# Which queue stores go out of: ScalarE's finished tiles on ScalarE's own DMA queue, in a hybrid attention and mLSTM encoder layer

## The chip, the cores and the metric

The kernel runs on one core of one Trainium2 chip. The metric is the device time of one execution in microseconds (us). The engines have these names in the profile: PE is TensorE (matmuls; PEld is its weight loads), DVE is VectorE, ACT is ScalarE, POOL is GpSimd, and SP is SyncE, which does no arithmetic here and only issues DMA transfers. "SPq" and "ACTq" are the sequencers of an engine: they wait, branch and issue transfers while the engine itself computes nothing.

## The reference

One encoder layer over two sequences, of 1024 and of 2048 tokens, each with the same 16 meta tokens ahead, at a model width of 1024:

```python
xn = _rmsnorm(h, g_pre)
proj = xn @ w_in + b_in.astype(xn.dtype)
na_q, na_k, na_v, na_z, ml_qk, ml_v, ml_z, ml_o, ml_g, mg = jnp.split(proj, SPLIT_IDX, axis=-1)
ya = _neighbourhood_attention(na_q.reshape(hd), na_k.reshape(hd), na_v.reshape(hd), na_rpb)
ya = (ya.reshape(B, L, NA_WIDTH) * jax.nn.silu(na_z)) @ w_a
yb = (_mlstm_branch(ml_qk, ml_v, ml_g, ml_o, ml_conv_w, ml_head_g) * jax.nn.silu(ml_z)) @ w_b
ga, gb = jnp.split(jax.nn.sigmoid(mg), 2, axis=-1)
y = (ga * ya + gb * yb) @ w_out
return h + _rmsnorm(y, g_post)
```

The projection is 1024 by 6672. The first branch is attention over a window of 8 by 16 grid positions, 8 heads of 64; the second a bidirectional mLSTM in chunks, 4 heads of 128. All is in float32.

## The kernel before

**Tiling.** A float32 product is made of three matmuls on a high and a low part of each operand (`mm3`, lines 144 to 146; written out by hand at lines 412 to 414 and 1304 to 1306). ACT makes the high part by a rounding copy, VectorE the low part as the difference. Tokens run in halves of 512. A projection column block is either feature-major (`fm_half` with `fm_evac`: 128 columns by 512 tokens) or token-major (`tm_unit` with `tm_store`: 128 tokens by 256 or 264 columns). Products gather in one of three `pj` banks of PSUM, are evicted to an SBUF tile (`st`, four buffers; `stT`, four buffers), and then stored to a scratch tensor in DRAM, from which a later stage loads them in its own layout.

**Two strands.** `dense` makes the projections and the final products in the order of `PLAN`; `sparse` makes the mLSTM and the attention of both sequences in the order of `STEPS`. `run` weaves them: each `yield` of the sparse strand has a price, and dense work of that price is put behind it. So TensorE's order is written out by hand, and between one step of the attention and the next stand dense matmuls that give ACT and VectorE time. In the profile the first mLSTM lies between about 300 and 780 us, the first attention from 780 to 1193, the second mLSTM from 1193 to 2015, the second attention from 2015 to about 2850; the final products (`final`) begin at about 1515 and end the span.

**Queues.** Only TensorE's order is fixed by hand. The instructions of the other engines are put in order by the framework's scheduler, and each engine takes its own in that order: an instruction that waits holds all behind it on its engine. The framework also sets all semaphore waits. Nearly every transfer, load or store, is issued by SP (2352 of them); POOL issues 14, for constants of the attention.

**The places of the change**, all of them stores of a tile whose last writer is ACT:

- `wpump`, line 240: a weight block is loaded once from the input, split by ACT (`hi`, line 233) and by VectorE or POOL (`lo`, line 236), used, and both parts are kept in DRAM for the next time that block is needed (loaded at line 231). 68 blocks.
- `fm_evac`, lines 348 and 350: mLSTM queries and keys (`MQ`, `MK`), written by line 343. The loads are at line 843. Where a half carries the meta tokens, these are stored for the other sequence too (line 350).
- `fm_evac`, line 356: attention queries (`NQ`, written by line 333), keys (`NK`, line 343), the attention's gate (`NZ`, which VectorE writes last, line 339) and the output gates (`GT`, line 341). They are loaded at lines 550, 633 and 1267.
- `tm_store`, line 452: the mLSTM's output gate `TO`, after ACT's tanh in place (line 451); loaded at line 1170.
- `ml_norm`, `turn`, line 1208: the mLSTM's normalised result `YB`, copied out of PSUM by ACT (line 1205); loaded at line 1245.

Other stores keep their queue: those of tiles that VectorE writes last (lines 241's low part, 439, 449, 456 to 468, 710, 918, 1111, 1377).

**The steps that the prediction speaks of.** The attention works on units of one head and 16 grid columns: scores (lines 664, 665), bias and row maximum (DVE, 668), exponential (ACT, 672), scaling (DVE, 681), transposes (PE, 689), split of the transposed weights (ACT 691, DVE 692), product with the values (PE, 701) and its eviction (ACT, 705). The loads of the next head (`na_prep`, lines 550 to 637, and the bias at line 606) are issued as a burst. The mLSTM's loads stand at lines 843, 889, 998 and 1005; its decay rows `um` (line 1005) are used by VectorE at line 1043; `ktl` (line 956) is the low part of its transposed keys. `mx` is the row maximum, `prb` the exponentials, `kd` the high part of the attention's keys.

Of the kernel before, what the change touches and what calls it, by code (L numbers as in the profile page):

```python
# [9 lines left out]
F32 = mybir.dt.float32  # L10
# [7 lines left out]
P = 128  # L18
# [3 lines left out]
NM = 16  # L22
# [7 lines left out]
C_NQ, C_NK, C_NV, C_NZ = 0, 512, 1024, 1536  # L30
C_MQ, C_MK, C_MV, C_MZ, C_MO, C_GA, C_GB = 2048, 2560, 3072, 3584, 4096, 4624, 5648
# [79 lines left out]
class K:  # L111
# [107 lines left out]
    def wpump(self):  # L219


        nc, wp = self.nc, self.wp
        self.wload()
        while self.wraw and self.wout < NBW:
            key, raw, nk, w = self.wraw.popleft()
            n = nk * w
            hi = wp.tile([P, 4 * WU], F32R, name="whi", bufs=NBW)
            lo = wp.tile([P, 4 * WU], F32R, name="wlo", bufs=NBW)
            if raw is None:
                for x, d in zip((hi, lo), self.wkept[key]):  # L230
                    nc.sync.dma_start(x[:, :n].bitcast(F32), d[:, :])
            else:
                nc.scalar.activation(hi[:, :n], raw[:, :n], AF.Copy)
                self.nu += 1
                eng = nc.vector if self.nu > 4 else nc.gpsimd
                eng.tensor_tensor(lo[:, :n], raw[:, :n], hi[:, :n].bitcast(F32), op=ALU.subtract)
                self.wkept[key] = []
                for x, part in ((hi, "h"), (lo, "l")):
                    d = self.dp.tile([P, n], F32, name=f"w{part}{len(self.wkept)}")
                    nc.sync.dma_start(d[:, :], x[:, :n].bitcast(F32))  # L240
                    self.wkept[key].append(d)
            self.wrdy.append([x[:, :n].rearrange("p (k c) -> p k c", k=nk) for x in (hi, lo)])
            self.wout += 1
            self.wload()
# [77 lines left out]
    def fm_evac(self, col, s, t0, meta, chunks, ps):  # L322

        nc, wp = self.nc, self.wp
        bi = (col // P) if col < 4608 else 36 + (col - 4624) // P
        bias = self.bfm[:, bi:bi + 1]
        st = wp.tile([P, HALF], F32, name="st", bufs=4)
        m = NM if meta else 0
        n = 512 + m
        for (c0, c1), p in zip(chunks, ps):  # L330
            o, q = st[:, c0:c1], p[:, :c1 - c0]
            if col < C_NK:
                nc.scalar.activation(o.rearrange("p (b r c) -> p r b c", r=8, b=4), q.rearrange("p (r b c) -> p r b c", r=8, b=4),
                                     AF.Identity, bias=self.bq8[:, bi:bi + 1], scale=0.125)
            elif C_NZ <= col < C_MQ:
                zb = wp.tile([P, HALF], F32, name="st", bufs=4)
                nc.scalar.activation(zb[:, c0:c1], q, AF.Identity, bias=bias)
                nc.scalar.activation(o, q, AF.Tanh, bias=self.bfh[:, bi:bi + 1], scale=0.5)
                nc.vector.scalar_tensor_tensor(o, o, 1.0, zb[:, c0:c1], op0=ALU.add, op1=ALU.mult)
            elif col >= C_GA:  # L340
                nc.scalar.activation(o, q, AF.Tanh, bias=self.bfh[:, bi:bi + 1], scale=0.5)
            else:
                nc.scalar.activation(o, q, AF.Identity, bias=bias)
        if C_MQ <= col < C_MV:
            dst = (self.MQ if col < C_MK else self.MK)
            h = (col % 512) // P
            lo = 0 if meta else NM + t0
            nc.sync.dma_start(dst[s][h][:, lo:lo + n], st[:, :n])
            if meta:
                nc.sync.dma_start(dst[1 - s][h][:, :NM], st[:, :NM])  # L350
            return
        if col >= C_GA:
            dst = self.GT[s][(col - C_GA) // P]
        else:
            dst = (self.NQ, self.NK, None, self.NZ)[col // 512][s][(col % 512) // P]
        nc.sync.dma_start(dst[:, t0:t0 + 512], st[:, m:n])
        if meta and C_NK <= col < C_NV:
            km = wp.tile([P, 64], F32, name="km", bufs=1)
            nc.gpsimd.memset(km, 0.0)
            nc.gpsimd.tensor_copy(km[:, 8:24], st[:, :NM])  # L360
            nc.gpsimd.tensor_copy(km[:, 32:48], st[:, :NM])
            nc.sync.dma_start(self.NKM[(col % 512) // P][:, :], km)
# [63 lines left out]
    def tm_store(self, col, wd, s, n, cnt, tok, st):  # L426
        nc, wp = self.nc, self.wp

        def rows(d, c0, c1, lo):
            return d[lo:lo + n * cnt, c0:c1].rearrange("(a p) c -> p a c", p=n)  # L430

        f = col % 512
        if C_MZ <= col < C_MO:
            th = wp.tile([P, 2, WU], F32, name="thT", bufs=1)
            nc.scalar.activation(th[:, :, :wd], st[:, :, :wd], AF.Tanh, scale=0.5)
            nc.vector.scalar_tensor_tensor(st[:, :, :wd], th[:, :, :wd], 1.0, st[:, :, :wd], op0=ALU.add, op1=ALU.mult)
            for a in range(2):
                nc.vector.tensor_tensor(st[:, a, :wd], st[:, a, :wd], self.hgt[:, 0, :], op=ALU.mult)
            nc.sync.dma_start(rows(self.SZ[s], f, f + wd, tok), st[:, :, :wd])
        elif col >= C_MO:  # L440
            c0 = col - C_MO
            no = min(wd, 512 - c0)
            if wd > no:
                g = wd - no
                if tok is None:
                    for q in range(2):
                        nc.sync.dma_start(self.GA[q][0:NM, :], st[:n, 0, no:wd])
                else:
                    nc.sync.dma_start(rows(self.GA[s], 0, g, NM + tok), st[:, :, no:wd])
            if tok is not None:  # L450
                nc.scalar.activation(st[:, :, :no], st[:, :, :no], AF.Tanh, scale=0.5)
                nc.sync.dma_start(rows(self.TO[s], c0, c0 + no, tok), st[:, :, :no])
        elif col >= C_MV:
            if tok is None:
                for q in range(2):
                    nc.sync.dma_start(self.MV[q][0:NM, f:f + wd], st[:n, 0, :wd])
            else:
                nc.sync.dma_start(rows(self.MV[s], f, f + wd, NM + tok), st[:, :, :wd])
        else:
            if tok is None:  # L460
                for lo in (8, 32):
                    nc.sync.dma_start(self.NVM[lo:lo + NM, f:f + wd], st[:n, 0, :wd])
            else:
                for a in range(cnt):
                    for r in range(2):
                        row = (tok + a * P) // 64 + r
                        dst = self.NV[s][:, row * 8:row * 8 + 8, f:f + wd]
                        nc.sync.dma_start(dst, st[r * 64:r * 64 + 64, a, :wd])
# [686 lines left out]
    def ml_norm(self, mp, s):  # L1155

        nc = self.nc
# [37 lines left out]
        def turn(i, e):  # L1195
            if i < 0:
                return
            hb = ld[i][e][0]
            if e == 0:
                rr[i] = mp.tile([P, 4, 2, P], F32, name="ybo", bufs=2)  # L1200
            yo = rr[i]
            pt = self.psum("tr", [P, 4, P])
            for h in range(4):
                nc.tensor.transpose(pt[:, h, :], hb[:, h], self.ident)
            nc.scalar.activation(yo[:, :, e, :], pt, AF.Copy)
            if e:
                for h in range(4):
                    nc.sync.dma_start(self.YB[s][h][:, 2 * P * i:2 * P * (i + 1)], yo[:, h].rearrange("p a b -> p (a b)"))
                ld.pop(i)
                rr.pop(i)  # L1210

# [2 lines left out]
        for i in range(N + 1):  # L1214
            if i < N:
                load(i + 1)
                yield from stats(i)
                yield A_N
            turn(i - 1, 0)
            if i < N:  # L1220
                norm(i, 0)
            yield A_N
            turn(i - 1, 1)
            if i < N:
                norm(i, 1)
            yield A_N
# [266 lines left out]
```

## Time and profile before

| | us |
|---|---|
| Median of three runs | 2937.11 (2936.93 to 2938.26) |
| The profiled execution's own time | 2935.2 |
| Its span, first to last instruction | 2933.4 |
| TensorE busy in the span | 2820.8 |
| ScalarE busy | 1288.7 |
| VectorE busy | 1747.6 |

A row of the list of groups or waits names an engine, a line, and a tile written and tiles read (`out<-in`, buffer numbers left out). A row of waits has in its end the total in us, how often, and the longest: `PE sm L701 <- DVE pts L692: 15.7, 12, 4.7` says that TensorE stood idle 12 times, 15.7 us in all, until line 692 had ended. `SPq L356 <- ACT st L341` is SP's sequencer, which could not issue line 356 before line 341 had ended. A row of a stage has its bounds and length, then busy us and instruction count of PE, PEld, DVE, ACT and POOL, then TensorE's granted clock, the busy share of the DMA engines and GB/s. A row for one line's issues has least, median and longest duration in ns, and first and last start. The chain in order of time has start, duration and what. A timeline row has start, duration, engine, line, operation, tiles and count, with the idle time before it and what ended that. The issue of a transfer is a row of SPq; its duration is that of issuing, not of the transfer, which goes on after it.

### The profile page before, as it was taken

Reading aid. Unit: us, or ns where it says so; the run is one execution under the profiler, and the core shown is the slowest. Engines: PE = TensorE matmul, PEld = TensorE weight load, DVE = VectorE, ACT = ScalarE, POOL = GpSimd, SP = SyncE. Lnnn points to the kernel's source line nnn. Section 1 sums busy time; section 2 is a strip of 40 time slices with the busy share of each in tenths; the row PEclk is TensorE's granted clock in tenths of the full one; section 3 lists DMA queues with packets and bytes.
Section 4 is the critical chain, followed back from the end, with each engine's and each line's share of the span. In section 5 each row is a group of like instructions: output and inputs, shape, how many; then the busy total and the mean of one; then the engine's idle time right before and its main releaser. Section 6 shows DMA issues by size and latency. Waiting matters only on the chain.

```text
span 2933.4 us, 49345 instructions
## 1 busy us (share of the span) xinstructions
PE 2820.8 (96%) x17488; PEld 2510.8 (86%) x17488; DVE 1747.6 (60%) x4722; ACT 1288.7 (44%) x3114; POOL 23.1 (1%) x107
## 2 busy tenths in 40 slices
PE   6999999999799999999999999989999999989998
PEld 6998898899689988888887998977888888879797
DVE  5233566556556665465568776565555557777843
ACT  4213546433344444456566554413444445435421
POOL 1000000000000000000000000000000000000000
PEclk9999999999899999999999999999999999999999
DMA  9655667656775654568679898488568658897875
GB/s 350 219 179 181 197 218 256 232 182 207 255 232 153 198 175 134 168 232 298 197 234 363 277 313 290 136 263 272 172 196 283 191 174 272 245 280 236 283 273 194
DMA packets 438760, 675.25 MB, mean 230 GB/s; under 512 B 52240, under 2 KB 253024, under 8 KB 438512
## 3 DMA queue, kind: packets, MB, share of 16 engines
q1 hardware_dynamic: 437392, 669.41, 70.1%
q0 software_dynamic: 1120, 2.69, 0.4%
q8 instruction: 137, 2.24, 0.3%
q14 instruction: 111, 0.91, 0.1%
HBM read 455.05 MB, written 216.90 MB: 229 GB/s over the span
## 4 chain that ended last, share of the span: by engine, by line
PE 83%; DMA 9%; DVE 5%; ACT 1%; issue 1%; SPq 1%; DVEq 0%; ACTq 0%
PE pj L144 15%; PE pj L145 15%; PE pj L146 15%; PE pj L412 6%; PE pj L413 6%; PE pj L414 6%; PE sm L701 3%; PE pj L1304 3%; PE pj L1306 3%; PE pj L1305 3%; PE tr L689 2%; DMA tg<-gt 2%; PE sc L665 1%; PE sc L664 1%; PE sm L146 1%; PE sm L145 1%
## 5 line engine op out<-in xcount | busy, mean ns | idle before, releaser
L144 PE MATMUL pj<-xh,whi 128*128 128x512 f32 (+1 forms) x1824 | 722.2, 396 | 2.4 <-DVE xl L310 2.2
L145 PE MATMUL pj<-xl,whi 128*128 128x512 f32 (+1 forms) x1824 | 701.3, 384 | 0.6 <-DVE xl L310 0.6
L146 PE MATMUL pj<-xh,wlo 128*128 128x512 f32 (+1 forms) x1824 | 699.8, 384 | 0.0
L412 PE MATMUL pj<-whi,xh 128*128 128x256 f32 (+3 forms) x1576 | 450.8, 286 | 0.0
L413 PE MATMUL pj<-wlo,xh 128*128 128x256 f32 (+3 forms) x1576 | 444.7, 282 | 0.0
L414 PE MATMUL pj<-whi,xl 128*128 128x256 f32 (+3 forms) x1576 | 444.2, 282 | 0.0
L146 PEld LDWEIGHTS pj<-xh,wlo 128*128 128x128 f32 x1824 | 344.6, 189 | 72.3
L144 PEld LDWEIGHTS pj<-xh,whi 128*128 128x128 f32 x1824 | 345.2, 189 | 57.3 <-DVE xl L310 2.6
L145 PEld LDWEIGHTS pj<-xl,whi 128*128 128x128 f32 x1824 | 345.9, 190 | 53.3 <-DVE xl L310 0.8
L412 PEld LDWEIGHTS pj<-whi,xh 128*128 128x128 f32 (+1 forms) x1576 | 294.3, 187 | 1.2
L413 PEld LDWEIGHTS pj<-wlo,xh 128*128 128x128 f32 (+1 forms) x1576 | 294.0, 187 | 1.1
L414 PEld LDWEIGHTS pj<-whi,xl 128*128 128x128 f32 (+1 forms) x1576 | 294.1, 187 | 0.9
L692 DVE TENSOR_TENSOR pts<-tr,pts 96x512 fp32r<-96x512 f32 (+2 forms) x192 | 132.2, 688 | 159.4 <-ACT pts L691 158.3
L672 ACT ACTIVATE prb<-sc,mx 128x384 f32<-128x384 f32 (+2 forms) x192 | 119.4, 622 | 238.2 <-DVE mx L668 234.1
L1304 PE MATMUL pj<-whi,mh 128*128 128x256 f32 x768 | 221.0, 288 | 0.4 <-DMA whi<-wh 0.4
L1306 PE MATMUL pj<-whi,mlo 128*128 128x256 f32 x768 | 217.6, 283 | 2.1 <-DVE mlo L1287 2.1
L1305 PE MATMUL pj<-wlo,mh 128*128 128x256 f32 x768 | 217.2, 283 | 0.0
L691 ACT ACTIVATE pts<-tr 96x512 fp32r<-96x512 f32 (+2 forms) x192 | 114.3, 595 | 170.0 <-PE tr L689 169.3
L421 DVE TENSOR_TENSOR stT<-pj,bb 128x256 f32<-128x256 f32 (+3 forms) x197 | 83.1, 422 | 145.3 <-PE pj L414 141.2
L144 PE MATMUL pj<-yh,whi 128*128 128x512 f32 x384 | 158.0, 412 | 11.0 <-DVE tg L1283 11.0
L668 DVE CUSTOM_DVE_ANT_1 sc<-sc,gt 128x384 f32<-128x384 f32 (+2 forms) x192 | 118.9, 619 | 73.2 <-PE sc L665 67.4
L146 PE MATMUL pj<-yh,wlo 128*128 128x512 f32 x384 | 153.4, 399 | 0.0
(234 smaller groups left out, 5067.5 us busy)
## 6 DMA issues: line engine op xcount, KB each, us to landing
whi<-wh SPq DMA_DIRECT2D x176, 512.0 KB
wlo<-wl SPq DMA_DIRECT2D x176, 512.0 KB
wh<-whi SPq DMA_DIRECT2D x64, 512.0 KB
wl<-wlo SPq DMA_DIRECT2D x64, 512.0 KB
wraw<-w_in SPq DMA_DIRECT2D x48, 512.0 KB
gt<-st SPq DMA_DIRECT2D x96, 256.0 KB
tg<-gt SPq DMA_DIRECT2D x96, 256.0 KB
xh<-xh SPq DMA_DIRECT2D x6, 2048.0 KB
```

The lines of the kernel that those rows point to most:

```text
L144: mm(out, ah, bh, start=start, stop=False)
L145: mm(out, ah, bl, start=False, stop=False)
L146: mm(out, al, bh, start=False, stop=stop)
L412: nc.tensor.matmul(o, xh, wh, start=k == 0, stop=False)
L413: nc.tensor.matmul(o, xh, wl, start=False, stop=False)
L414: nc.tensor.matmul(o, xl, wh, start=False, stop=k == KT - 1)
L668: nc.vector.tensor_tensor_reduce(out=so, in0=so, in1=gt[:, g0:g0 + ns, c0:c0 + 32], op0=ALU.add, op1=ALU.min, scale=-1.0, scalar=3.0e38, a ...
L672: nc.scalar.activation(pr_[:, :N].rearrange("p (b a c) -> p b a c", b=4, c=8), sc[:, :N].rearrange("p (a b c) -> p b a c", b=4, c=8), AF.E ...
L692: nc.vector.tensor_tensor(pts[:ks, :, 1, :], pt[:ks], pts[:ks, :, 0, :].bitcast(F32), op=ALU.subtract)
L1304: nc.tensor.matmul(o, mh[:, k, xs], wh, start=k == 0, stop=False)
L1305: nc.tensor.matmul(o, mh[:, k, xs], wl, start=False, stop=False)
L1306: nc.tensor.matmul(o, ml[:, k, xs], wh, start=False, stop=k == KT - 1)
```

## The change

Six stores call `nc.scalar.dma_start`, so that ACT's sequencer issues them into ACT's own queue, in the place of `nc.sync.dma_start`. In `wpump` only the high part moves. In `fm_evac` the attention's gate `NZ` (columns `C_NZ` to `C_MQ`) stays with SP, and so does the meta keys' tile `km`. The tiles, the transfers and all arithmetic stay.

```diff
-                    nc.sync.dma_start(d[:, :], x[:, :n].bitcast(F32))
+                    (nc.scalar if part == "h" else nc.sync).dma_start(d[:, :], x[:, :n].bitcast(F32))
...
+        q = nc.sync if C_NZ <= col < C_MQ else nc.scalar
         if C_MQ <= col < C_MV:
...
-            nc.sync.dma_start(dst[s][h][:, lo:lo + n], st[:, :n])
+            q.dma_start(dst[s][h][:, lo:lo + n], st[:, :n])
             if meta:
-                nc.sync.dma_start(dst[1 - s][h][:, :NM], st[:, :NM])
+                q.dma_start(dst[1 - s][h][:, :NM], st[:, :NM])
             return
...
-        nc.sync.dma_start(dst[:, t0:t0 + 512], st[:, m:n])
+        q.dma_start(dst[:, t0:t0 + 512], st[:, m:n])
...
                 nc.scalar.activation(st[:, :, :no], st[:, :, :no], AF.Tanh, scale=0.5)
-                nc.sync.dma_start(rows(self.TO[s], c0, c0 + no, tok), st[:, :, :no])
+                nc.scalar.dma_start(rows(self.TO[s], c0, c0 + no, tok), st[:, :, :no])
...
-                    nc.sync.dma_start(self.YB[s][h][:, 2 * P * i:2 * P * (i + 1)], yo[:, h].rearrange("p a b -> p (a b)"))
+                    nc.scalar.dma_start(self.YB[s][h][:, 2 * P * i:2 * P * (i + 1)], yo[:, h].rearrange("p a b -> p (a b)"))
```

By the counts of the profile of before these are 340 transfers: 68 at line 240, 48 at 348, 8 at 350, 144 at 356, 24 at 452 and 48 at 1208.

## The prediction

> **What bounds the kernel now.** I read the page's head and chain first, then the busy time by stage, then TensorE's own waits.
>
> ```profile
> span 2933.4 us, 49345 instructions
> PE 2820.8 (96%) x17488; PEld 2510.8 (86%) x17488; DVE 1747.6 (60%) x4722; ACT 1288.7 (44%) x3114; POOL 23.1 (1%) x107
> PE 83%; DMA 9%; DVE 5%; ACT 1%; issue 1%; SPq 1%; DVEq 0%; ACTq 0%
> ```
> ```profile
> 0.00:60.00 60.00, 36.72 (x272) 35.55 (x273) 35.11 (x70) 28.35 (x50) 8.56 (x22) 0.97 0.98 337
> 1340.00:1950.00 610.00, 591.22 (x3519) 521.45 (x3519) 409.80 (x1166) 320.13 (x880) 3.58 (x18) 0.99 0.78 260
> 2015.00:2456.00 441.00, 439.38 (x2197) 364.95 (x2197) 243.83 (x589) 210.27 (x443) 1.02 (x2) 1.00 0.68 210
> 2456.00:2933.00 477.00, 444.68 (x2853) 401.27 (x2852) 316.15 (x766) 178.38 (x452) 1.02 (x2) 0.97 0.80 256
> ```
>
> TensorE is busy for 96% of the span and carries 83% of the chain. Its idle time is 2933.4 - 2820.8 = 112.6 us: 23.3 in the first 60 us (almost all before the first real product), 32.3 after 2456, and about 57 between. The moved stores end at 2456 (the last output-gate store), so the last 32.3 us can change only through another order of the other engines' work. ACT, the fourth busy time of a stage row, is at most 320.13 / 610 = 52% busy in these rows: it has room, but it stands between TensorE's products and TensorE's next operands. A microsecond that TensorE loses is not won back, so what counts is which waits in front of it shrink or grow.
>
> ```profile
> PE pj L307 <- DVE xr L296: 22.5, 2, 18.2
> PE tr L1204 <- DVE hn L1193: 15.9, 2, 10.0
> PE sm L701 <- DVE pts L692: 15.7, 12, 4.7
> PE sc L664 <- ACT kd L644: 15.0, 2, 14.1
> PE sm L146 <- DVE ktl L956: 3.8, 5, 1.6
> ```
>
> The start (L307) and the normalisation (L1204) wait for loads that no moved store stands in front of for long. The attention's start (L664, one wait of 14.1 us) does have one in front.
>
> **What the change removes.** Out of SP's queue go 340 transfers: 68 high weight halves (L240), 48 + 8 mLSTM query and key stores (L348, L350), 48 attention query and key and 96 gate stores (L356), 24 of L452 and 48 of L1208. SP waits in order, so each held up whatever load stood behind it until ACT had written:
>
> ```profile
> SPq L356 <- ACT st L341: 77.4, 33, 7.0
> SPq L356 <- ACT yg L705: 52.6, 13, 7.4
> SPq L240 <- ACT whi L233: 46.8, 22, 5.5
> SPq L348 <- ACT st L343: 35.8, 17, 6.9
> ```
>
> That is 212.6 us of queue time in four rows. The 46.8 us do not go away: the low half stays on SP and is written later, by VectorE. Most of the rest is time in which SP had nothing urgent; TensorE sees it only where the chain runs through SP behind such a store. The chain in order of time shows two places:
>
> ```profile
> 778.88 1.20 SPq L348
> 780.13 1.26 SPq L550
> 781.44 10.67 DMA qr<-nq
> ...
> 1209.41 0.32 SPq L356
> 1210.25 4.65 DMA va<-mv
> ```
>
> At 778.88 the key store is issued and only then the first query load of the attention, whose landing ends the 14.1 us wait. Without the store the load goes 1.2 us earlier, perhaps 3 if its other condition (the buffers freed by the last L1208 stores) is met by then. At 1209.41 the same shortens the mLSTM's start by 0.4 to 1 us. For the start and for VectorE's late decay rows I allow another 2 us. Gain taken: 6 us; bounds 0 and 20, the latter a third of the 57 us of idle time between 60 and 2456.
>
> A rule speaks against more. The Trainium skill, DMA: Bandwidth & Descriptors, section Issuing engines are not separate DMA queues, says that transfers issued by different engines share the same 16 DMA engines and interleave, so that a second issuer saves only the time of issuing. By it the gain would be the 1.20 and 0.32 us of issue above and no more, and the sum below would be some 4 us higher; it does not count waiting in order, which the four rows show. That two queues share the engines no run here shows yet.
>
> **What it adds to ACT: issue time.** A store now takes ACT's sequencer, at SP's rate by the nearest rows (least, median and longest in ns):
>
> ```profile
> L356 SPq DMA_DIRECT2D gt<-st x96: 319/324/1465, 1343.8 to 2456.4; - x96
> L240 SPq DMA_DIRECT2D wh<-whi x68: 319/360/3507, 16.1 to 1634.7; - x68
> L348 SPq DMA_DIRECT2D mq<-st x24: 319/392/1523, 46.2 to 865.5; - x24
> L1208 SPq DMA_DIRECT2D yb<-ybo x48: 314/438/1233, 740.4 to 2015.3; - x48
> ```
>
> 144 x 0.324 + 68 x 0.360 + 80 x 0.392 + 48 x 0.438 = 124 us (the other stores of L356, and those of L348, L350 and L452, put at the medians of these rows). ACT goes from 44% to 48% of the span; bounds 340 x 0.314 = 107 us, and 420 us if each took as long as the 1.233 us of the slowest L1208. On TensorE's path I put 2 us: between an eviction and ACT's next due work there is usually a gap of over 1 us, which hides 0.4. If that cover is gone, the stall shows in the attention first (below).
>
> **What it adds to ACT: waiting.** The store needs ACT's own result, which is there at once, and also a free place among the transfers under way. SP's queue shows that second condition: its issues wait for landings with which they have no data in common.
>
> ```profile
> SPq L550 <- DMA whi<-wh: 13.7, 10, 2.4
> SPq L1245 <- DMA gt<-st: 3.5, 2, 1.8
> ```
>
> On SP such a wait held loads; on ACT it holds every activation behind it: the attention's exponentials (L672), its transposes' splits (L691) and outputs (L705), the mLSTM's splits, and the other evictions, for which TensorE's `pj` banks wait. It bites when SP has just sent a burst. Two such places, SP and ACT (VectorE and TensorE below them) side by side:
>
> ```profile
> 800.65 1.08 SPq L550 DMA_DIRECT2D kr<-nk  x2
> 807.54 0.38 SPq L348 DMA_DIRECT2D mk<-st  x1
> 801.15 0.69 ACT L343 ACTIVATE st<-pj,bfm 128x512 f32<-128x512 f32 x1 [4.17 <-PE pj L146]
> 802.47 0.58 ACT L672 ACTIVATE prb<-sc,mx 128x384 f32<-128x384 f32 x1 [0.63 <-DVE mx L668]
> ```
> ```profile
> 2225.44 4.37 SPq L265 DMA_DIRECT2D xl<-xl  x2
> 2236.31 0.33 SPq L356 DMA_DIRECT2D gt<-st  x1
> 2230.23 0.67 ACT L341 ACTIVATE st<-pj,bfh 128x512 f32<-128x512 f32 x1
> 2232.89 0.60 ACT L691 ACTIVATE pts<-tr 128x512 fp32r<-128x512 f32 x1 [1.70 <-PE tr L689]
> 2233.52 0.69 DVE L692 TENSOR_TENSOR pts<-tr,pts 128x512 fp32r<-128x512 f32 x1 [1.70 <-ACT pts L691]
> 2235.94 0.63 PE L701 MATMUL sm<-pts,vt 128*128 128x256 f32 x4
> ```
>
> The tile stored at 807.54 was written by 801.84; the one stored at 2236.31 by 2230.90. If ACT waits as long as SP's queue took, L672 moves from 802.47 to 807.92 (5.4 us late, and TensorE has no other reserve there: the chain goes through it), and L691 from 2232.89 to 2236.64, 3.75 late; its VectorE half ends at 2234.21, 1.73 before TensorE takes it, so TensorE loses 2.0. Part of these delays was SP's own order, which ACT does not inherit, so half is nearer: 2.7 and 1.0, mean 1.9. How often does a store meet that?
>
> ```profile
> L356 SPq DMA_DIRECT2D gt<-st x61: 319/323/1465, 2016.0 to 2449.2; - x61
> L606 SPq DMA_DIRECT2D gt<-rpb x20: 332/333/1565, 2022.7 to 2442.2; - x20
> ```
>
> In the attention from 2015 to 2456 there are 61 gate stores and twenty bursts of head loads (one L606 load each), and about thirty stores of L348 and L356 stand beside the first attention, some 93 in all. How many fall behind a burst no row counts; one in fifteen is an estimate: a burst of the kind above comes every 22 us, and only stores in its last microseconds wait long. 6 x 1.9 = 11 us. For the other 247 stores ACT has more distance to TensorE; I take 4 us, of the size of the 3.8 us that TensorE now waits for `ktl`. Together 15, bounds 0 (the order puts the store behind the urgent activation each time) and 50 (one store in three of the 93, at the same 1.9 us, is 59, less what overlaps).
>
> **The sum.** -6 + 2 + 15 = +11 on the span of 2933.4, 2944 us. The profiled execution took 2935.2 and the median of the runs is 2937.11, 3.7 over the span; so 2948 us, 0.4% slower.
>
> **The rivals.** *Freed loads win.* SP runs ahead of the stores, loads come some microseconds earlier, and ACT's places are free when it asks. For it: the 212.6 us of waiting, and the largest waits of TensorE end in landings. Against it: most of these waits have no moved store in front. Price: 15 of the 57 us of idle time come back and ACT's two terms are near 0, 2937 - 15 = 2922; it decides if ACT's stores find a free place in over nine of ten cases in the attention.
>
> *Hidden on both sides.* The stores were ready when SP reached them and ACT is 56% idle: -6 against +2 and +4, 2937. For it: ACT's 1% of the chain. Against it: the 1.7 us of reserve at L701 is short.
>
> *ACT becomes late everywhere.* The upper bound of the wait and a new order of evictions: one store in three behind a burst in the attention, and the `pj` banks waiting for late evictions outside it: +50 + 2 - 6, 2983. For it: the longest issue of 3.5 us in the first 60 us, where DMA is 98% busy. Against it: ACT's 48 to 52%.
>
> *It does not do what it says.* If SP's later transfers wait for the landing of ACT's store anyway (the L1245 row waits for `gt<-st`), the load gains only a few places in the order: the gain falls to 0 and the sum is 2954, inside the forecast's range.
>
> **How the numbers follow.** Forecast with the fourth case 0.47, freed loads 0.25, hidden 0.16, late everywhere 0.12. The forecast's own range is 2940 to 2965. The whole range reaches from 2920 to 2985: below it nearly half of the freed loads' chance is left out, 0.1, above it half of the last case's, 0.06. What a measurement of this kernel can tell from no change is about 0.2%, 5.9 us: faster (under 2931) 0.24, within 0.20 (the hidden case and the edges of both neighbours), slower (over 2943) 0.56.
>
> **What would show it.** Right: SP's waits for L341, L343 and L451 are gone; ACT's sequencer shows about 340 issues of 0.3 to 0.45 us, and waits for landings of loads; TensorE's waits for L692 (15.7 us) rise by about ten, the 14.1 us wait at L664 falls by 1 to 3. Wrong: TensorE's idle time falls below 112.6 us; or it rises in the tail after 2456, where nothing was moved, which would mean that the order of the work, not the queues, decided; or ACT's issues take over 1 us each.

## The result and the profile after

| | before | after |
|---|---|---|
| Median, us | 2937.02 (2924.82 to 2938.26, 4 runs) | 2962.45 (2957.01 to 2965.71, 4 runs) |
| Span of the profiled execution, us | 2933.4 | 2955.2 |
| TensorE idle in the span, us | 112.6 | 125.8 |

The ratio is 1.0098 with a 95% interval of 1.0081 to 1.0114, about 1% slower; by the medians it is 25 us. The page of the kernel after, its head and its second DMA queue (packets, MB, share of the 16 DMA engines):

```profile
span 2955.2 us, 49082 instructions
PE 2829.4 (96%) x17488; PEld 2515.5 (85%) x17488; DVE 1745.4 (59%) x4722; ACT 1289.5 (44%) x3114; POOL 23.0 (1%) x107
...
q10 hardware_dynamic: 52032, 98.78, 9.1%
```

The change does what it says: 98.78 MB now go out of a second queue. The work is the same (the same 17488 matmuls in the same order, ACT's busy time within 1 us), so the time lies in waits and in a slower TensorE. Its idle time grew by 13.2 us and its busy time by 8.6. Below line 344 the lines of the kernel after are one higher than those of before.

TensorE's waits after, total us, times, longest:

```profile
PE pj L307 <- DVE xr L296: 22.3, 2, 15.9
PE sm L702 <- DVE pts L693: 18.7, 15, 3.4
...
PE sc L665 <- ACT kd L645: 13.1, 1, 13.1
PE sc L144 <- ACT qh L1024: 5.1, 1, 5.1
...
PE pj L307 <- ACT st L343: 3.1, 1, 3.1
...
PE sm L144 <- ACT kth L956: 3.0, 1, 3.0
```

The reader should look for rows that have no counterpart in the list of before: one wait of 5.1 us for `qh`, one of 3.0 for `kth`, and the 1.2 us for `st` at the start grown to 3.1. All three name ACT. The last of them stood in the list of before as:

```profile
PE pj L307 <- ACT st L343: 1.2, 1, 1.2
```

The wait for the second half of the attention's split weights (L693, was L692) rose only from 15.7 to 18.7.

ACT's own waits, of which the following end in the landing of a transfer that the waiting instruction does not use:

```profile
ACT st L337 <- DMA yb<-ybo: 25.2, 4, 9.0
...
ACT qh L1024 <- DMA xl<-xl: 10.5, 1, 10.5
...
ACT pts L692 <- DMA xh<-xh: 6.9, 1, 6.9
ACT cv L853 <- DMA xh<-xh: 6.9, 1, 6.9
...
ACT st L343 <- DMA xl<-xl: 5.8, 1, 5.8
...
ACT st L343 <- DMA xh<-xh: 5.1, 1, 5.1
```

`qh` splits the mLSTM's queries; `xl` and `xh` are the two parts of a half of the input, saved to DRAM at line 317 and loaded back at line 265. Before, no row of this list has ACT waiting for `xh` or `xl`. What stands between is a store. Two stretches of ACT and SP in order of time (start, duration, engine and line):

```profile
1328.56 0.49 SPq L265 DMA_DIRECT2D xl<-xl  x1
1329.14 1.69 SPq L265 DMA_DIRECT2D xh<-xh  x2
1330.88 2.52 SPq L265 DMA_DIRECT2D xl<-xl  x1
...
1334.10 0.69 ACT L341 ACTIVATE st<-pj,bfh 128x512 f32<-128x512 f32 x1 [1.40 <-PE pj L146]
1344.89 0.33 ACTq L357 DMA_DIRECT2D gt<-st  x1
1345.32 0.42 ACT L1024 ACTIVATE qh<-cv 128x256 fp32r<-128x256 f32 x1 [10.52 <-DMA xl<-xl]
...
2242.12 5.09 SPq L265 DMA_DIRECT2D xl<-xl  x2
2246.77 0.27 ACT L706 ACTIVATE yg<-sm 64x128 f32<-64x128 f32 x1
2253.62 0.33 ACTq L357 DMA_DIRECT2D gt<-st  x1
2253.99 0.60 ACT L692 ACTIVATE pts<-tr 128x512 fp32r<-128x512 f32 x1 [6.95 <-DMA xh<-xh]
```

The gate tile is written by 1334.79, and the store could go; it goes at 1344.89, when a part of a kept half has landed that SP sent for just before (four transfers of 1 MB in some 5 us). For 10.1 us ACT does nothing. The issue itself takes 0.33 us. Counting every store on ACT's sequencer that starts over 1 us after ACT's previous instruction ended, I find 30 of 340, 104 us in all, the first at 15.58, the last at 2263.16 us.

Only few of these reach TensorE. The start of each matmul after, less the start of the same matmul before, gives a curve. It has four upward steps: +6.3 in the first 60 us, +7.3 at 1342, +6.0 at 1790 and +8.2 at 2239 to 2244. They sum to 27.8; small drops between them and after 2456, 6 us in all, leave the 21.8 of the span. The last three steps lie at the reload of a kept half, the first at the saves of the first half.

### The profile page after: what moved, and what is told of

It reads as the page before. It is cut to its first block, busy times and chain, and to the rows that moved or that the text cites. A ratio compares the mean times of both kernels' runs of the same rounds, so it can differ in the third digit from the quotient of the medians.

```text
span 2955.2 us, 49082 instructions
## 1 busy us (share of the span) xinstructions
PE 2829.4 (96%) x17488; PEld 2515.5 (85%) x17488; DVE 1745.4 (59%) x4722; ACT 1289.5 (44%) x3114; POOL 23.0 (1%) x107
## 3 DMA queue, kind: packets, MB, share of 16 engines
q10 hardware_dynamic: 52032, 98.78, 9.1%
## 5 line engine op out<-in xcount | busy, mean ns | idle before, releaser
L693 DVE TENSOR_TENSOR pts<-tr,pts 96x512 fp32r<-96x512 f32 (+2 forms) x192 | 132.1, 688 | 164.7 <-ACT pts L692 160.5
L692 ACT ACTIVATE pts<-tr 96x512 fp32r<-96x512 f32 (+2 forms) x192 | 114.5, 596 | 174.0 <-PE tr L690 156.4
L144 PE MATMUL pj<-yh,whi 128*128 128x512 f32 x384 | 158.7, 413 | 13.1 <-DVE tg L1284 13.1
```

Of the source, the lines that this page charges most:

```text
L144: mm(out, ah, bh, start=start, stop=False)
L693: nc.vector.tensor_tensor(pts[:ks, :, 1, :], pt[:ks], pts[:ks, :, 0, :].bitcast(F32), op=ALU.subtract)
```

## The experiments

Twelve kernels were run, four at a time on one chip, each against the kernel before on that chip (2930.42, 2929.99 and 2930.11 us median for the three groups). This table sums up the steps: each number is the lateness in us, against the profiled execution of before, of the same matmul at that time. All kernels have TensorE's order unchanged. A single profile drifts by some microseconds, up to 9, in small steps, as e4 shows, whose median is within 0.2% of before; a step between neighbouring columns is the surer reading. The profiled execution of e6 is the fastest of its nine (2931.19 us, against a median of 2940.65), so its column shows less than its median does.

```
at (us of before)            60   1193   1300   1360   1750   1850   2200   2300   2456
after                       6.3    3.4    2.3    9.6    9.8   15.8   15.3   23.5   23.5
e1_reload_pool              6.9    7.5    7.0    7.2    7.1    7.2    7.1   16.8   16.8
e1b_before_reload_pool      1.4   -0.8   -1.1   -1.1   -0.9   -0.8   -2.2   -2.2   -2.2
e3_issue_time_only          1.0    3.3    1.6    1.6    3.8    3.8    1.2    1.2    1.2
e4_stores_pool              1.8    5.4    7.8    7.8    9.1    9.1    4.4    4.4    4.4
e5_gates_only              -0.4   -0.4   -1.8    5.8    7.2    7.2    6.5   14.2   14.2
e6_all_but_gates            6.9    2.0    0.7    0.7    0.3    4.4    2.6    2.6    2.7
e7_eight_back               3.2   -1.0   -1.6   -1.6   -1.7   -1.7   -2.9    6.5    6.5
e8_weights_only             1.2    1.7    0.9    0.9    2.5    2.5    0.5    0.5    0.5
e9_windows_on_sp           -0.3   -0.4   -0.5   -0.5    0.6    0.6    0.8    0.8    0.8
e10_windows_on_act          7.1    7.4    9.6   16.7   16.9   23.3   22.3   30.9   30.9
e11_small_reloads           5.6    4.4    2.9    9.0    8.6   10.3    8.6   15.0   15.0
e12_before_small_reloads    1.6    0.2    1.1    1.1    2.6    2.6    0.4    0.4    0.4
```

### Is it the landings of the reloads?

The kernel after, with the reload of kept halves issued by POOL; and the same edit on the kernel before as a control.

```diff
-                    nc.sync.dma_start(x[-1][:, k:k + 4, :512].bitcast(F32), part[:, k:k + 4, :])
+                    nc.gpsimd.dma_start(x[-1][:, k:k + 4, :512].bitcast(F32), part[:, k:k + 4, :])
```

> The changed kernel, but the four-megabyte reloads of kept halves (line 265, 24 transfers of 1 MB) are issued by POOL. Theory (ACT is held by stores that wait for the landing of an unrelated transfer, worst behind these reloads): the three steps of TensorE's delay at about 1342, 1790 and 2238 us of before, 7.3 + 5.2 + 7.6 = 20 us, go away: 2942 to 2946 us. Rival, issue time on ACT: nothing changes, 2957 to 2965. Rival, another order of the other engines: no forecast, but the three steps would not go all at once.

> The kernel before with the same reloads from POOL: the control for the run beside it. All theories: 2937 plus or minus 6, since SP's reloads showed no wait of TensorE; whatever it differs is the price of the move of the reloads alone.

Measured: 2946.47 us, ratio 1.0054 (1.0035 to 1.0073); the control 2932.18, 1.0004 (0.9991 to 1.0017). The steps at 1342 and 1790 are gone (7.0 to 7.2 and 7.1 to 7.2 in the table), so it was the landing of the reloads that held ACT there. The third step stays. ACT in this kernel, in order of time:

```profile
2238.57 0.68 ACT L341 ACTIVATE st<-pj,bfh 128x512 f32<-128x512 f32 x1
2248.78 0.33 ACTq L357 DMA_DIRECT2D gt<-st  x1
2249.15 0.60 ACT L692 ACTIVATE pts<-tr 128x512 fp32r<-128x512 f32 x1 [9.61 <-DMA whi<-wh]
```

A weight reload holds the same store now. Nothing ties the hold to line 265: another transfer that SP has sent and that is slow to land can do it.

### Is it ACT's issue time, or the second queue?

The kernel before with every store left on SP, and two one-column ACT copies for each stored tile in place of the issue; and the kernel after with the 340 stores on POOL's queue.

```diff
+                    if part == "h":
+                        for _ in range(2):
+                            nc.scalar.activation(self.warm, x[:, :1].bitcast(F32), AF.Copy)
...
+        if not C_NZ <= col < C_MQ:
+            for _ in range(4 if C_MQ <= col < C_MV and meta else 2):
+                nc.scalar.activation(self.warm, st[:, n - 1:n], AF.Copy)
```
```diff
-        q = nc.sync if C_NZ <= col < C_MQ else nc.scalar
+        q = nc.sync if C_NZ <= col < C_MQ else nc.gpsimd
```

> The kernel before, all stores on SP, but ACT runs two one-column copies of the stored tile behind each of the 340 stores: some 0.3 to 0.45 us of ACT time per store that needs the tile's last write, and no wait for a transfer. Rival, issue time on ACT: 2955 to 2965, like the change. Theory of waits: 2937 to 2942.

> The same 340 stores go out of POOL's queue in the place of ACT's. POOL is 1% busy. Theory of waits: ACT is never held, SP is freed as in the change: the steps at 1342, 1790 and 2238 are gone, and what is left is the gain of SP's freed queue, 2925 to 2940. Rival, second queue's traffic delays the loads: 2955 to 2965 as in the change, since the traffic is the same.

The page's head of the first of them:

```profile
PE 2819.5 (96%) x17488; PEld 2509.7 (86%) x17488; DVE 1746.8 (60%) x4722; ACT 1396.7 (48%) x3794; POOL 23.2 (1%) x107
```

ACT is busy for 108 us more than before, about what 340 issues at 0.33 us take, and the time is 2931.2 us, ratio 1.0008 (0.9994 to 1.0023): issue time costs nothing that can be measured. With the stores on POOL it is 2933.14, 1.0011 (0.9998 to 1.0024). That run removes the same stores from SP and sends the same bytes from a second place, and neither gains nor loses: the freed SP queue brings nothing, and a second source of the same traffic costs nothing. What is left as the cost is the hold on ACT. The run does not show that POOL can afford such a hold, for there it has none: in its trace a store on POOL starts a median of 0.3 us after ACT's write and, but for the first (3.7 us), at most 2.2 us after it. Where SP's time went is in its waits, after:

```profile
SPq L231 <- PE pj L146: 234.3, 64, 17.7
SPq L607 <- DVE mx L669: 182.2, 35, 18.1
```

The waits for L341, L343 and L451 (now L452) are gone from the list, and those for other things are longer: the bias load at L607 (L606 before) waited 81.6 us for the row maximum before, the weight reload at L231 203.9. SP arrives earlier and waits there for its buffers.

### Which of the stores?

On the kernel before, a part of the change alone: only the 96 gate stores; all but these; only the 68 weight halves. And the kernel after with eight stores put back on SP. The cuts show `fm_evac` against the kernel after, for the gates alone, for all but the gates and for the stores put back. The first of these kernels also leaves the weights and the stores of lines 453 and 1209 on SP, and the last also the first four weight halves; weights alone leaves all but the weights on SP.

```diff
-        q = nc.sync if C_NZ <= col < C_MQ else nc.scalar
+        q = nc.scalar if col >= C_GA else nc.sync
```
```diff
-        q = nc.sync if C_NZ <= col < C_MQ else nc.scalar
+        q = nc.sync if C_NZ <= col < C_MQ or col >= C_GA else nc.scalar
```
```diff
+        if q is nc.scalar:
+            k = C_MQ <= col < C_MV
+            self.cnt[k] += 1
+            if self.cnt[k] in ((33, 65, 113), (1,))[k]:
+                q = nc.sync
```

> Of the 340 moved stores only the 96 gate stores go out of ACT's queue. Theory (a few long holds behind kept-half reloads make the loss): the gates carry two of the four large steps of the delay curve, +7.3 us at 1342 and +7.7 at 2238, so +12 to +18 us, 1.004 to 1.006. Rival (the loss grows with the number of stores): 96 of 340 times 25 us = +7 us, 1.0024. Rival (the other stores' holds matter as much in the attention): under +5.

> All moved stores but the 96 gate stores go out of ACT's queue (244). Theory: the steps at 42 to 48 us (+6) and at 1790 (+5) remain, less the 3 us won back at 310: +6 to +11 us, 1.002 to 1.004. Rival (in proportion): +18 us, 1.006.

> Only the 68 high weight halves go out of ACT's queue. Theory: holds only in the first 60 us, where SP sends its largest bursts: +3 to +6 us, 1.001 to 1.002, all of it before 60 us in the delay curve. Rival (the start's loss comes from the mLSTM query stores that follow): 0, 1.000.

> The changed kernel with eight of its 340 stores back on SP's queue: the first four weight halves, the first mLSTM query store, and the stores that ACT issued at 1344.9, 1796.7 and 2253.6 us. Theory (these holds make the loss): at most 8 us over the kernel before, 1.000 to 1.003. Rival (a hold only passes to the next store, since the burst is still there): +18 us or more, 1.006. Rival (many small losses): +24, 1.008.

Measured: gates alone 2946.89 us, 1.0063 (1.0050 to 1.0077); all but the gates 2940.65, 1.0041 (1.0026 to 1.0056); weights alone 2932.49, 1.0013 (1.0001 to 1.0024); eight put back 2941.13, 1.0046 (1.0030 to 1.0062).

The two parts of the change add up to it (0.63% and 0.41% against 0.98%), and each carries its own steps in the table: the gates those at 1342 and 2240 and none at the start, the rest those at the start and at 1790. Both ratios came out just above the range expected; by the medians, 16.9 and 10.7 us, they are inside it. The weights alone cost at the edge of what can be measured, and not where the theory put it: by the table 1.2 us at 60, where 3 to 6 were expected. So the weights by themselves do not make the start's loss; whether the mLSTM stores do without the weights was not run.

The stores put back are nine transfers, since the first mLSTM query tile carries the meta tokens and is stored twice. They are 3% of the 340 and carry half of the loss, more than a share by number and less than I expected. Two steps are gone and the first is halved, but the last one is still there. In this kernel (lines of L341 and L357 are L342 and L363 here, L1024 is L1030):

```profile
1331.88 0.42 ACT L1030 ACTIVATE qh<-cv 128x256 fp32r<-128x256 f32 x1 [0.93 <-PE tr L145]
...
1336.85 0.69 ACT L342 ACTIVATE st<-pj,bfh 128x512 f32<-128x512 f32 x1 [0.76 <-PE pj L146]
1337.43 0.41 ACT L1039 ACTIVATE kh<-kf 128x256 fp32r<-128x256 f32 x1
1346.00 0.33 ACTq L363 DMA_DIRECT2D gt<-st  x1
1346.37 0.72 ACT L1079 ACTIVATE sh<-um 128x256 fp32r<-128x256 f32 x2 [8.53 <-DMA raw<-mk]
```

At 1346 the hold has passed to the next store, as the rival said, and is still 8.2 us long; but `qh` and `kh` were written before it, and TensorE does not notice. At 2244 it passed to the next store too, with an 8.9 us hold, and there it cost 9.4 us. So two things must meet: a store behind a burst, and work due on ACT within the length of the hold.

### The places alone, both ways

39 stores: the first 8 weight halves, the stores of the first 8 mLSTM query tiles (12), and 19 of L357 around the three reloads. On SP in the kernel after; and alone on ACT, with the other 301 on SP.

```diff
+            c = self.cnt[k]
+            held = c <= 8 if k else 33 <= c <= 38 or 65 <= c <= 67 or 108 <= c <= 117
+            q = nc.sync if held else nc.scalar
```

> The changed kernel with 39 of its 340 stores back on SP: the first 8 weight halves, the stores of the first 8 mLSTM query tiles (12), and 19 stores of L357 around the three reloads of kept halves, so that a hold cannot pass to a neighbour. Theory (a hold costs only where ACT's next work is due, and these are the places): 0 to +6 us, 1.000 to 1.002. Rival (the burst holds whichever ACT store comes next): +12 us or more, 1.004.

> The reverse: only these 39 stores go out of ACT's queue, 301 stay on SP. Theory: nearly the whole loss, +18 to +27 us, 1.006 to 1.009. Rival (it is the number of stores on ACT, in proportion): 39 of 340 times 28 us = +3 us, 1.001.

Measured: 2933.57 us, 1.0006 (0.9993 to 1.0019) with the 39 on SP, and 2958.41, 1.0094 (1.0076 to 1.0111) with only them on ACT. 39 stores make the whole loss (28 us, a little above the range expected), the other 301 none that can be measured. TensorE's waits in the second, where `qh` is L1031 and `kth` L963:

```profile
PE pj L308 <- ACT st L344: 5.5, 2, 4.6
PE sc L144 <- ACT qh L1031: 4.4, 1, 4.4
PE sm L144 <- ACT kth L963: 3.4, 1, 3.4
```

These are the three new rows of the kernel after, from 39 stores. The 301 are not free of holds: in the first kernel I count 21 issues that start over 1 us late, 54 us in all, the longest 11.4. They stand where ACT's next instruction waits for a load in any case, or where TensorE has other work. On SP the wait is there too, and TensorE does not see it. The first kernel (gate store L364, head loads L558) has at the place of the last step:

```profile
2225.97 4.91 SPq L266 DMA_DIRECT2D xl<-xl  x2
...
2237.00 0.68 ACT L342 ACTIVATE st<-pj,bfh 128x512 f32<-128x512 f32 x1
2239.75 0.45 SPq L558 DMA_DIRECT2D kr<-nk  x1
2242.56 1.74 SPq L558 DMA_DIRECT2D kr<-nkm  x2
...
2244.93 0.59 ACT L699 ACTIVATE pts<-tr 128x512 fp32r<-128x512 f32 x1
2245.92 6.86 SPq L364 DMA_DIRECT2D gt<-st  x3
```

The gate tile written by 2237.68 is stored at 2245.92, 8.2 us later. In between SP stands until the landings of two parts of the reload (its issues at 2239.75 and 2242.56) and of two later loads, while ACT goes on, to the next eviction and to the split for TensorE at 2244.93. The 6.86 us of the last row are no hold: the third of its stores waits for an eviction that ends at 2252.43.

### How long a hold is

The kernel after with each reload cut from 4 transfers of 1 MB into 16 of 256 KB, and the same on the kernel before.

```diff
-                for k in range(0, KT, 4):
-                    nc.sync.dma_start(x[-1][:, k:k + 4, :512].bitcast(F32), part[:, k:k + 4, :])
+                for k in range(0, KT):
+                    nc.sync.dma_start(x[-1][:, k:k + 1, :512].bitcast(F32), part[:, k:k + 1, :])
```

> The changed kernel with each reload of a kept half (4 transfers of 1 MB, L265) cut into 16 of 256 KB, same bytes. Theory A (ACT is held until one particular large transfer has landed): fewer bytes are under way ahead of a store, the steps at 1342, 1790 and 2238 fall to half or less, 1.003 to 1.006. Theory B (ACT waits for the backlog of bytes in the DMA engines, however cut): as the changed kernel, 1.009 to 1.011.

> Control: the kernel before with the same 16 small transfers. Both theories: 0.999 to 1.002; SP pays 12 more issues of about 0.33 us a reload, off TensorE's path.

Measured: 2949.17 us, 1.0063 (1.0046 to 1.0080); the control 2929.43, 1.0000 (0.9987 to 1.0013). By the ratio a third of the loss went, which is theory A's side of the middle, though just above its range. The holds themselves went from 10.1 to 8.0 us, from 6.4 to 4.6 and from 6.6 to 6.7, which is nearer to theory B.

Which landing a store waits for stands in the trace's records of the semaphores, which the views leave out. A semaphore is a counter that a transfer raises as it lands. The transfers of SP and ACT share eight of them in turn: in the kernel before, each of the eight has 294 of SP's 2352 transfers. In all 30 late stores of the kernel after, ACT first waits on the semaphore that the store itself is about to use, until the transfer that used it last has landed; the store goes 0.02 to 0.4 us after that landing. In 24 of the 30, seven other transfers of SP and ACT were issued between the two. The gate store of 1344.89 shares its semaphore with the reload sent at 1330.88, whose landing is recorded at 1344.81. POOL's transfers use eight other semaphores, and of the 340 stores on POOL (e4) 319 wait for none of the eight of SP and ACT.

So both theories have a part. One particular transfer is waited for, as in A, chosen by the order of issue and not by its data; and when it lands depends on what is under way ahead of it, as in B: with the small reloads the gate store of 1343.71 waits for a piece of 256 KB that was sent at 1337.65 and landed at 1343.64. An estimate from the rows of the next section: 4 MB at the 386 GB/s of that stretch take 10.9 us, about the longest of the three.

No version beat the kernel before by more than can be measured.

## Why the prediction was right, and where its sizes were off

The forecast was slower, 2948 us, by ACT being held until unrelated transfers land; it was slower by that mechanism, 2962.45, inside the range but near its upper end: the loss of 25 us is over twice the 11 forecast. The "free place among the transfers under way" is the semaphore of the last experiment. By its steps:

- *The gain, -6.* Failed: it is about 0 (e4, 1.0011). The 14.1 us wait at the attention's start did fall, to 13.1, as forecast (1 to 3 less). But the prediction took the wait of a later load behind a store for time that SP could give to TensorE, and SP's freed time went into other waits of its own, for buffers. The rival "freed loads win" falls with it; the Trainium skill's rule (DMA: Bandwidth & Descriptors, Issuing engines are not separate DMA queues), which left only issue time to gain, was nearer for this term, though it says nothing of what the second issuer loses by waiting.
- *Issue time, +2.* Too much, if anything: 0 within the error (e3). An issue on ACT took 0.33 us as estimated:

```profile
L240 ACTq DMA_DIRECT2D wh<-whi x68: 326/326/396, 15.6 to 1644.2; - x68
```

- *Waiting, +15.* The term that was mis-sized: with the others at 0, the whole loss is it, 13.2 us as idle time of TensorE and the rest as a slower clock behind the waits (below). That 13.2 is near 15 is luck, for the places are others. The prediction spread the term over some six holds of 1.9 us in the attention, and 4 us for the 247 other stores. There are instead four places, with waits of TensorE of 3.0 to 5.1 us and steps of 6 to 8 us by the curve, and only one lies in the attention. Two steps of its working made it small. It halved the delay seen on SP (5.4 and 3.75 us) because part of that was SP's own order, which ACT would not inherit; the holds on ACT were 10.1, 6.4 and 6.6 us, and ACT does inherit that order, since its store waits for a transfer that SP sent some eight places before. And the stores outside the attention had "more distance to TensorE": the part of the change without the gates costs 0.41%, 12 us. The reason is the reload of kept halves, which the prediction quoted for 2225 us and did not follow to its other places, and the saves of the first half at the start.
- *TensorE's waits.* L692 was to rise by ten: 3.0. The rest came as waits for `qh`, `kth` and `st`, which were not named.
- *The tail.* It was to stay, and did not grow:

```profile
2015.00:2456.00 441.00, 434.70 (x2157) 360.13 (x2156) 238.38 (x602) 202.85 (x427) 1.02 (x2) 0.99 0.67 208
2456.00:2933.00 477.00, 453.35 (x2866) 405.98 (x2865) 318.77 (x738) 190.26 (x470) 1.02 (x2) 0.99 0.82 262
```

TensorE's idle time after 2456 is 23.7 us here and 32.3 before; in the attention ahead of it 6.3 and 1.6. The stretch holds work from some 20 us earlier in the program, so I don't read the fall as a gain. By the curve the lateness goes from 23.5 at 2456 to 21.8 at the end. None of the three signs that would have made the prediction wrong appeared: TensorE's idle time rose, the tail did not carry it, and no line's issues had a median over 0.4 us on ACT.

- *The other rivals.* "Hidden on both sides" is what e9 shows of 301 stores. "Late everywhere" fails: holds are in many places, but late evictions stop TensorE only at the start (the row for `st`, 3.1 us) and once more for 0.6 us.

What the sum lacked altogether is 8.6 us of longer busy time. The clock shows it, in stretches around the four holds:

```profile
49.20:52.60 3.40, 3.40 (x16) 3.17 (x17) 0.50 (x1) 1.57 (x3) 0.00 (x0) 0.51 0.99 323
...
1330.00:1342.80 12.80, 10.65 (x56) 8.69 (x54) 3.99 (x11) 3.39 (x11) 0.00 (x0) 1.00 1.06 386
1342.80:1349.80 7.00, 4.02 (x12) 3.36 (x13) 3.87 (x13) 3.44 (x10) 0.00 (x0) 0.51 1.08 364
...
1800.30:1807.20 6.90, 5.93 (x18) 4.97 (x19) 4.54 (x13) 3.91 (x12) 0.00 (x0) 0.51 0.98 328
...
2254.20:2261.00 6.80, 5.63 (x17) 4.74 (x18) 2.57 (x7) 2.02 (x5) 0.00 (x0) 0.50 1.06 336
```

The wait of 5.1 us ends at 1345.8. From 1342.8, still within it, the granted clock is 0.51 for 7 us. The 4.02 us of work in that stretch would have taken some 2.0 less at full clock: 5.1 + 2.0 is 7.1 of the 7.3 of the step. At 2254 it is 3.4 us of wait, 2.8 of clock and a second wait of 1.1, 7.3 of the 8.2. The same sum gives 3.1 + 1.7 of 6.3 at the start and 3.0 + 2.9 of 6.0 at the step of 1790. The four clock terms add up to 9.4, about the 8.6 of busy time.

The Trainium skill, TensorE: Matmul & The Clock Gate, section Part 1: The HAM clock gate, says that the array's clock is halved once TensorE has been idle for a window of about 3.4 us, and restored after such a window of sustained work. The trace agrees on the half (0.50 and 0.51). On the length it is shorter here: a wait of 3.0 us was enough at 1800.

## What to carry to other kernels

A store on a compute engine's queue is an instruction that can wait for other transfers, and all that engine's work waits behind it; on SP, which computes nothing here, the same wait was free. Look at which transfers share a semaphore: the store is held by the last one that used its own, whatever the data and whichever engine sent it. Before moving stores, look for the bursts of the queue that stays (here reloads of 1 MB pieces) and ask what the new issuer has due within ten microseconds of a store that follows one. A wait of an otherwise full TensorE costs more than its length, since the half clock that came with it added 2.0 us to 5.1 and 2.8 to 3.4 here.

## What was not expected of the hardware

A store whose data were ready stood on ACT's sequencer for up to 11.6 us, 35 times its issue of 0.33 us. The longest, in the kernel after, between the eviction and the next work of ACT:

```profile
783.99 0.69 ACT L343 ACTIVATE st<-pj,bfm 128x512 f32<-128x512 f32 x1 [2.96 <-PE pj L146]
796.28 0.33 ACTq L349 DMA_DIRECT2D mk<-st  x1
797.26 0.63 ACT L640 ACTIVATE stk<-qr 128x512 fp32r<-128x512 f32 x1 [12.58 <-DMA qr<-nq]
```

It costs nothing, since the attention's first split stands behind it and waits for the query load `qr` in any case. And the second queue moved no more bytes a second than the one alone: 386 GB/s at a busy share of 1.06 in the stretch of the step at 1342 (above), of which ACT's queue carried 41, and before, at the same place:

```profile
1333.00:1343.00 10.00, 10.00 (x57) 8.62 (x56) 5.86 (x19) 5.54 (x15) 0.00 (x0) 1.00 1.05 393
```

Where ACT's queue carried more, 157 GB/s from 1380 to 1390 us in the kernel after, the two together moved 377 at the same share of 1.06. This agrees with the rule of the Trainium skill cited above (DMA: Bandwidth & Descriptors, Issuing engines are not separate DMA queues): the 16 DMA engines are shared.
